# Gate, up and down as seven block products in place of eight, in three stages

## The chip, the cores and the metric

The kernel runs on one core of a Trainium2 chip. Such a core has a matmul engine, TensorE (PE in the profile; its weight loads, which overlap the matmuls, are PEld), and VectorE (DVE), ScalarE (ACT), GpSimd (POOL) and SyncE (SP), which run side by side, each through its own list of instructions in order, and wait for each other by semaphores. Operands lie in SBUF (128 partitions), matmuls write into PSUM (eight banks of 128 x 512 values), and 16 DMA engines move data between SBUF and DRAM. The metric is device time of one call in microseconds, the median of several runs.

## The reference

One layer of a decoder, for 2048 new prompt tokens and 8 decode tokens, all in float32. Two mixers (window attention and gated linear attention, GLA) give `mix` of 1024 columns; then comes what the change touches, with D_MODEL 1024 and D_FF 2816:

```python
def finish(x, o_attn, o_gla, r_gla, gla_norm_g, w_o, ffn_norm_g, w_gate, w_up, w_down):
    ...
    h = x + jnp.concatenate([o_attn.astype(x.dtype), g], axis=-1) @ w_o
    z = rmsnorm(h, ffn_norm_g)
    return h + (jax.nn.silu(z @ w_gate) * (z @ w_up)) @ w_down
```

## The kernel before

Every large product is made in three passes (`mm3`, lines 94 to 97): each float32 operand is split (`split`, L84 a cast on ACT, L85 a subtraction on DVE) into a high and a low part in a format of fewer bits that PE takes at its full rate, and high x high, high x low and low x high are added up in PSUM. So each operand that PE reads costs one ACT and one DVE pass over it, weights at every load.

The order of instructions on each engine is set by a scheduler ahead of time, from the order of the program and its own estimate of durations. A tile's buffer comes from a pool with a fixed number of them, so a load or a split waits until the last reader of an earlier tile is done. All loads and stores are issued from SP, whose list is in order too: a transfer that waits holds up those behind it.

The program has three phases.

*Phase A* makes the projections and window attention of 16 blocks of 128 tokens. *Phase B* is GLA, in eight rounds of two blocks: `front_b` (projections) and `gla_b` (the recurrence), and at the end of each block `mob`, the block's normalised output, is written to `mix_d` in DRAM (L853). Beside the last round runs `mixer_out_0` (L903): the first superblock's (512 tokens) product with `w_o`, into PSUM tiles `ps_wo`, added to x (`add_h`, L566), normalised, transposed by PE (`norm_T`) and split into `zT`. Its weights are loaded at L914.

*Phase C* (from L960) goes over four superblocks of 512 tokens; the decode tokens ride with the first, so that its columns are taken in `HALVES` of 256 and 264. D_FF is 22 blocks of 128, taken in `GROUPS` of 8, 8 and 6. For each group, `gate_up` (L1040) makes for each block the transposed products `pg` and `pu` (8 k tiles x 3 passes each, 512 columns), silu on ACT (L1057), the product on DVE (L1058) and the split `mid`; then `down` (L1065) multiplies `mid` with `w_down` into `ps_nat` and adds to `ht`, which holds h. For the first superblock `down_0` makes the product transposed (`ps_yT`) and `finish_0` turns it back (L1122). Between the two, in the last group, `mixer_out` makes h and `zT` of the next superblock. `unit` (L978) loads 512 KB of weights and splits them (tiles `wrc` and `hl`); gate, up and down are loaded again for each superblock.

Of the kernel before, what the change touches and what calls it, by code (L numbers as in the profile page):

```python
# [35 lines left out]
HALVES = ((0, 256), (256, 520))  # L36
GROUPS = ((0, 8), (8, 16), (16, 22))
# [7 lines left out]
def hymba_kernel(ctx: ExitStack, tc: tile.TileContext, I, O, X=None, phases=3):  # L45
# [25 lines left out]
    # the decode tokens' high parts in columns 0..7, low parts in columns 32..39  # L71
# [15 lines left out]
    def fold(ps, w, pool):  # L87
        """Sum of the two parts of a stacked decode product -> [8, w] in SBUF."""
# [5 lines left out]
    def mm3(ps, lh, ll, rh, rl, start, stop):  # L94
        nc.tensor.matmul(ps, lh, rh, start=start, stop=False)  # L95
        nc.tensor.matmul(ps, lh, rl, start=False, stop=False)  # L96
        nc.tensor.matmul(ps, ll, rh, start=False, stop=stop)  # L97
# [8 lines left out]
    def rstd_fast(ss, n, scale, cols):  # L106
        """(scale * ss + EPS) ** -0.5 by ln and exp, then one Newton step."""
# [26 lines left out]
    # ------------------------------------------------------------------ phase A  # L134
    with ExitStack() as ph:
# [21 lines left out]
        # resident projection weights of q_a k_a v_a lr, as exact high and low parts  # L157
# [30 lines left out]
        # per-partition gains of the transposed q and k  # L188
# [27 lines left out]
        def dense_dec(W, c0, c1):  # L216
            """The decode tokens' products: both parts of n stacked, two passes."""
# [8 lines left out]
        def gate_r(ps, n):  # L226
            """silu(r) of n tokens, with exp and ln only."""
# [10 lines left out]
        def head_norm(ps, n, c0, heads):  # L238
            """RMSNorm factors of the heads of 64 columns that start at column c0."""
# [7 lines left out]
        def norm_q(pq, n):  # L247
            r = head_norm(pq, n, 0, 8)
            qn = wk.tile([P, 512], F32, tag="qn", name="qn")
            # heads in the order (chunk, kv): chunk c holds heads c and 4 + c  # L250
# [25 lines left out]
        def project(b):  # L276
# [10 lines left out]
            # [v0 high, v0 low, v1 low, v1 high]  # L287
# [13 lines left out]
            # kv group 0: high rows 0..63, low rows 64..127; kv group 1 the other way round  # L301
# [84 lines left out]
        def decode_a():  # L386
            with ExitStack() as decs:
# [25 lines left out]
                # slots 0..126 hold the cached keys 1.., slot 127 the new key  # L413
# [69 lines left out]
        def make_bias():  # L483
            """Relative-position bias with the band mask, Toeplitz over (query, key)."""
            with tc.tile_pool(name="a_ext", bufs=1) as ep:
# [12 lines left out]
                # the queries in reverse order, turned round by a permutation  # L498
# [48 lines left out]

    # z^T of a superblock; in phase B its columns hold n^T of an even and of an odd pair of blocks
    late = pool(ctx, "late", 1, side="right")
    zT = late.tile([P, 2, KD, 520], F32R, name="zT")  # L550
    h_d = [dram.tile([P, D], F32, name=f"h_d{i}") for i in range(4)]
    hdec_d = dram.tile([ND, D], F32, name="hdec_d")
    w_o = I["w_o"][0]
# [640 lines left out]
```

## Time and profile before

| | us |
|---|---|
| median of three runs | 2439.91 (2439.74 to 2440.58) |
| span of the profiled execution | 2436.4 |
| median less span | 3.5 |
| first product with `w_o` starts | 721.1 |
| first gate product starts | 793.75 |
| last add of `down` starts | 2432.74 |

The profile is of one execution, and the runs' time holds some 3.5 us outside its span. In a row of a group stand its line, engine, operation, what it writes and reads, shapes and count, then its busy time and the mean of one in ns, and last the idle time of the engine before such instructions, with what ended it. In a row of a window stand start and end, its length, the busy time of PE, PEld, DVE, ACT and POOL with the number of instructions, the granted clock, the DMA engines' share and GB/s. In a timeline stand start, duration, engine and line; SPq is SP's issuing of transfers. Matmuls overlap each other: one of 512 columns is shown with 0.39 us, though they start some 0.23 us apart.

### The profile page before, as it was taken

The page shows a single profiled execution, that of the slowest core. Times are in us where ns is not written, and L with a number is a line of the kernel's source. Part 1 is how long each engine was busy: PE and PEld are TensorE (multiplying, and loading weights), DVE is VectorE, ACT ScalarE, POOL GpSimd, SP SyncE. Part 2 cuts the span into 40 slices and gives each one's busy share as a digit, 9 for nine tenths or more (in the row PEclk, how much of TensorE's full clock was granted, in tenths as well). Part 3 has the DMA queues.
Part 4 walks back from the last instruction along what each step waited for, and adds up shares of the span by engine and source line. Part 5 has one row for each costly group of instructions (what it writes and reads, how often), then busy time and mean ns, then how long its engine had stood idle before and what let it go on. Part 6 is the DMA issues. An engine that isn't in the chain of part 4 may idle for free.

```text
span 2436.4 us, 33308 instructions
## 1 busy us (share of the span) xinstructions
PE 2384.0 (98%) x13129; PEld 2039.6 (84%) x13129; DVE 1189.5 (49%) x2238; ACT 860.4 (35%) x1676; POOL 375.2 (15%) x460
## 2 busy tenths in 40 slices
PE   8998898999999999999999999999999999999999
PEld 6887787888887999999888888888888888888887
DVE  6886687787677433333443333353333334333332
ACT  5766677343343322222222222232222223222221
POOL 2543443654562000000000000000000000000000
PEclk9999999999999999999999999999999999999999
DMA  6423335433243523323454323354232333333231
GB/s 210 138 84 106 98 115 179 156 105 129 68 143 121 182 93 124 97 87 96 147 165 129 95 96 95 95 173 147 95 95 95 92 97 123 95 96 91 95 92 68
DMA packets 316636, 280.76 MB, mean 115 GB/s; under 512 B 11623, under 2 KB 263792, under 8 KB 314416
## 3 DMA queue, kind: packets, MB, share of 16 engines
q1 hardware_dynamic: 316480, 278.64, 36.4%
q8 instruction: 103, 1.69, 0.3%
q14 instruction: 53, 0.43, 0.1%
HBM read 228.80 MB, written 50.84 MB: 115 GB/s over the span
## 4 chain that ended last, share of the span: by engine, by line
PE 87%; DVE 5%; DMA 3%; POOL 2%; issue 1%; ACT 1%; SPq 0%; DVEq 0%; ACTq 0%; POOLq 0%
PE ps_nat L96 7%; PE ps_nat L95 7%; PE ps_nat L97 7%; PE pg L95 7%; PE pu L95 7%; PE pg L97 7%; PE pu L97 7%; PE pg L96 7%; PE pu L96 7%; PE ps_d L95 3%; PE ps_d L97 3%; PE ps_d L96 3%; PE ps_yT L95 2%; PE ps_yT L96 2%; PE ps_yT L97 2%; POOL bd L765 2%
## 5 line engine op out<-in xcount | busy, mean ns | idle before, releaser
L85 DVE TENSOR_TENSOR hl<-wrc,hl 128x1024 fp32r<-128x1024 f32 (+1 forms) x290 | 353.2, 1218 | 695.5 <-ACT hl L84 694.7
L84 ACT CAST hl<-wrc 128x1024 fp32r<-128x1024 f32 (+1 forms) x290 | 301.9, 1041 | 741.0 <-PE ps_nat L97 313.5
L95 PE MATMUL pg<-zT,hl 128*128 128x512 f32 (+2 forms) x880 | 308.7, 351 | 0.0
L95 PE MATMUL pu<-zT,hl 128*128 128x512 f32 (+2 forms) x880 | 308.3, 350 | 0.0
L97 PE MATMUL pg<-zT,hl 128*128 128x512 f32 (+2 forms) x880 | 308.0, 350 | 0.0
L97 PE MATMUL pu<-zT,hl 128*128 128x512 f32 (+2 forms) x880 | 308.0, 350 | 0.0
L96 PE MATMUL pg<-zT,hl 128*128 128x512 f32 (+2 forms) x880 | 307.0, 349 | 0.0
L96 PE MATMUL pu<-zT,hl 128*128 128x512 f32 (+2 forms) x880 | 306.8, 349 | 0.0
L103 POOL TENSOR_TENSOR rs_r<-rs_v,nhalf 128x1 f32<-128x1 f32 (+3 forms) x51 | 43.4, 855 | 1325.5 <-DVE rs_v L102 1324.8
L96 PE MATMUL ps_nat<-hl,mid 128*128 128x512 f32 x528 | 209.0, 396 | 0.0
L95 PE MATMUL ps_nat<-hl,mid 128*128 128x512 f32 x528 | 208.5, 395 | 0.0
L97 PE MATMUL ps_nat<-hl,mid 128*128 128x512 f32 x528 | 204.2, 393 | 0.0
L1058 DVE TENSOR_TENSOR sg<-sg,pu 128x512 f32<-128x512 f32 (+1 forms) x110 | 64.1, 583 | 251.5 <-PE pu L97 250.5
L96 PEld LDWEIGHTS pu<-zT,hl 128*128 128x128 f32 x880 | 165.4, 188 | 23.9
L97 PEld LDWEIGHTS pu<-zT,hl 128*128 128x128 f32 x880 | 165.4, 188 | 24.0
L97 PEld LDWEIGHTS pg<-zT,hl 128*128 128x128 f32 x880 | 165.4, 188 | 23.9
L96 PEld LDWEIGHTS pg<-zT,hl 128*128 128x128 f32 x880 | 165.4, 188 | 23.8
L95 PEld LDWEIGHTS pg<-zT,hl 128*128 128x128 f32 x880 | 165.4, 188 | 22.9
L95 PEld LDWEIGHTS pu<-zT,hl 128*128 128x128 f32 x880 | 165.2, 188 | 22.9
L1057 ACT ACTIVATE sg<-pg 128x512 f32<-128x512 f32 (+1 forms) x110 | 56.5, 514 | 353.8 <-PE pg L97 353.8
L765 POOL TENSOR_TENSOR bd<-E,qTb 64x128 f32<-64x128 f32 x224 | 127.2, 568 | 69.1 <-ACT E L753 54.2
L95 PEld LDWEIGHTS ps_nat<-hl,mid 128*128 128x128 f32 x528 | 99.0, 188 | 24.1
(347 smaller groups left out, 4758.0 us busy)
## 6 DMA issues: line engine op xcount, KB each, us to landing
wrc<-in_w_gate_dram SPq DMA_DIRECT2D x88, 512.0 KB
wrc<-in_w_up_dram SPq DMA_DIRECT2D x88, 512.0 KB
wrc<-in_w_down_dram SPq DMA_DIRECT2D x86, 512.0 KB
nT_d<-nT SPq DMA_DIRECT2D x16, 1024.0 KB
zT<-nT_d SPq DMA_DIRECT2D x8, 2048.0 KB
mt<-mix_d SPq DMA_DIRECT2D x12, 1024.0 KB
xt<-in_x_prompt_dram SPq DMA_DIRECT2D x16, 512.0 KB
mix_d<-mo SPq DMA_DIRECT2D x16, 512.0 KB
```

Of the source, the lines that this page charges most:

```text
L84: nc.scalar.copy(h, src)
L85: (eng or nc.vector).tensor_tensor(l, src, h.bitcast(F32), ALU.subtract)
L95: nc.tensor.matmul(ps, lh, rh, start=start, stop=False)
L96: nc.tensor.matmul(ps, lh, rl, start=False, stop=False)
L97: nc.tensor.matmul(ps, ll, rh, start=False, stop=stop)
L103: nc.gpsimd.tensor_tensor(r[:n, :cols], v[:n, :cols], nhalf[:n, :cols], ALU.pow)
L765: nc.gpsimd.tensor_tensor(bv[rows, :, h], eo, qo, ALU.mult)
L1057: nc.scalar.activation(sg[:, :w], pg[:, :w], AF.Silu)
L1058: nc.vector.tensor_tensor(sg[:, :w], sg[:, :w], pu[:, :w], ALU.mult)
```

## The change

Gate, up and down are each taken as a product of 2 x 2 blocks, by the Winograd form of Strassen's algorithm: seven products of sums of blocks, P1 to P7, in place of eight. The sums of activations are made once and kept, those of weights for each use, and the results are put together by adds. What was interleaved becomes three stages behind phase B. Phases A and B keep their work; `mixer_out_0` is gone from B.

*Stage M.* `w_o` is loaded once and stays split in SBUF (WO). Tiles of 128 tokens go in the order 0, 4, 1, 5 and so on: product, add, h to DRAM (`h_d`, L981), normalisation (with `rstd`, whose power is on POOL), transposes. For each two tiles that are four apart `operands` makes four sums and seven splits (`zhl`) and writes each, 512 KB in runs of 512 bytes, to `zc_d` by a DMA that POOL issues (L1016).

*Stage G.* Two superblocks of 1024 tokens, whose two blocks of rows are 512 tokens wide each (516 in the second, where the decode tokens ride, in two pieces of 258). The seven operands z are loaded once for a superblock (L1199, 2.1 MB each). For each of 11 pairs of D_FF blocks, gate and up have seven products of 4 k tiles x 3 passes each. `load_w` brings 4 x 512 KB of weights, `sums_a` their sums, `units` the splits (`whl`, seven buffers). `Strassen.ready` takes each finished product out of PSUM: P1 is copied by ACT; P6, P7, P5, P4 and P3 are added by DVE to what is there. P2 is added in PSUM onto P1, P7 and P4 onto P6, P3 onto P5; the eight banks go as three, three and two (tags a, b, c). In the first superblock gate's and up's products alternate; in the second all seven of gate come first. Four adds and subtractions make the seven operands of mid, which POOL writes to `md_d` (256 KB each, L1193).

*Stage D.* The pairs are taken in groups of 3, 3, 3 and 2. The 21 units of weights of a group are split once and kept (22 buffers). For each of eight pairs of row tiles the seven mid operands are loaded (`mr`, L1267) and split, and the four results of 128 x 512 are added to `h_d` in DRAM by a DMA with an add, which POOL issues; in the last group h is loaded (L1274), added, and written out. The decode tokens have products of their own (88 matmuls).

The diff, cut to what is new (`mixer_out_0` and the whole of phase C go, and the buffer of `zT` is now inside phase B):

```diff
-HALVES = ((0, 256), (256, 520))
-GROUPS = ((0, 8), (8, 16), (16, 22))
+GROUPS = ((0, 3), (3, 6), (6, 9), (9, 11))
+WIDTHS = (512, 516)
+PIECES = (((0, 512),), ((0, 258), (258, 516)))
+PRODS = ("P1", "P6", "P2", "P7", "P5", "P4", "P3")
...
-        mixer_out_0()
...
+        def operands(sb, mt, b):
...
+            sub(t1, b12, b11)
+            sub(t2, b22, t1)
+            sub(t3, b22, b12)
+            sub(t4, b21, t2)
+            for q, src in enumerate((b11, t2, b21, t3, t1, t4, b22)):
+                hl = hlp.tile([P, 2, 4, 132], F32R, tag="hl", name="zhl")
+                split(hl[:, 0, :, :w], hl[:, 1, :, :w], src)
+                nc.gpsimd.dma_start(zc_d[sb][q][:, :, :, mt * P:mt * P + w], hl[:, :, :, :w].bitcast(F32))
...
+    def sums_a(a11, a12, a21, a22):
+        yield a11
...
+        sub(x, a11, a21)
+        sub(y, a22, x)
+        yield y
+        yield a12
+        yield x
+        add(x, a21, a22)
+        yield x
+        yield a22
+        sub(y, a12, y)
+        yield y
...
+    BANK = {"P1": "a", "P2": "a", "P6": "b", "P7": "b", "P4": "b", "P5": "c", "P3": "c"}
...
+            if q == "P1":
+                nc.scalar.copy(p1, ps)
+            elif q == "P6":
+                add(u2, ps, p1)
+            elif q == "P7":
+                add(u3, ps, p1)
+            elif q == "P5":
+                add(u3, ps, u3)
+                self.done("22", i, u3)
+            elif q == "P4":
+                add(p1, ps, p1)
+                self.done("21", i, p1)
+            elif q == "P3":
+                add(u2, ps, u2)
+                self.done("12", i, u2)
+            elif q == "P2":
+                self.done("11", i, ps)
...
+            def prod(st, q, hl):
+                z = zc[q]
+                hv = hl.rearrange("p s (k n) -> p s k n", k=4)
+                for i, (c0, c1) in enumerate(pieces):
+                    ps = st.bank(q, i)[:, :c1 - c0]
+                    for k in range(4):
+                        mm3(ps, hv[:, 0, k], hv[:, 1, k], z[:, 0, k, c0:c1], z[:, 1, k, c0:c1],
+                            q in ("P1", "P6", "P5") and k == 0, k == 3, q not in ("P1", "P6", "P5"))
+                    st.ready(q, i)
...
+            add(s1, m12, m22)
+            sub(s2, s1, m11_)
+            sub(s3, m11_, m12)
+            sub(m12, m21, s2)
+            g = next(g for g, (p0, p1) in enumerate(GROUPS) if p0 <= fp < p1)
+            for q, src in enumerate((m11_, s2, m21, s3, s1, m22, m12)):
+                nc.gpsimd.dma_start(md_d[sb][g][:, :, q, fp - GROUPS[g][0], :], src.rearrange("p (m t) -> p m t", m=4))
...
+                    if last:
+                        add(hq[which], c, hq[which])
+                        nc.gpsimd.dma_start(O["y_prompt"][0, ti * P:(ti + 1) * P, cols], hq[which])
+                        return
+                    if which == "11":
+                        nc.scalar.copy(c11, c)
+                        c = c11
+                    nc.gpsimd.dma_start(h_d[ti][:, cols], c, accum_op=ALU.add)
```

Three places show how the engines' lists change. The first is SP's list at the end of phase B, before: `mix_d<-mob` writes a finished block, `wro` is a load of `w_o`, `zT<-mix_d` loads mix of a tile, `h_d<-ws` stores h.

```order
L853 DMA mix_d_83<-mob 256x1x512
L914 DMA wro<-in_w_o_dram 128x2x512
L914 DMA wro<-in_w_o_dram 64x2x512 x4
L914 DMA wro<-in_w_o_dram 128x2x512
L909 DMA zT<-mix_d_74 128x16x128
L914 DMA wro<-in_w_o_dram 128x2x512
L909 DMA zT<-mix_d_75 128x16x128
L725 DMA r<-r_d_113 128x512
L853 DMA mix_d_84<-mob 256x1x512
```

The same place after the change, from the last but one block on:

```order
L863 DMA mix_d_86<-mob 256x1x512
L922 DMA out_gla_state_prompt_dram<-Sbd 64x128 x2
L967 DMA h<-in_x_prompt_dram 128x1024 x2
L863 DMA mix_d_87<-mob 256x1x512
L955 DMA wro<-in_w_o_dram 64x2x512 x4
L955 DMA wro<-in_w_o_dram 128x2x512 x2
```

The loads of `w_o` stood ahead of the last four blocks' writes; now they stand behind the last of them.

The second is POOL's list in the middle of stage M. Before, POOL's list ends with the last rows of phase B (`qk`, `kd`), and behind them it has only the powers of the normalisations:

```order
L782 TENSOR_TENSOR qk<-qTb,kTb 128x512
L799 TENSOR_TENSOR kd<-kd,kTb 128x512
L103 TENSOR_TENSOR rs_r<-rs_v,nhalf 128x4 x2
L103 TENSOR_TENSOR rs_r<-rs_v,nhalf 128x1 x4
L103 TENSOR_TENSOR rs_r<-rs_v,nhalf 8x1
L103 TENSOR_TENSOR rs_r<-rs_v,nhalf 128x1 x12
```

After, for two tiles (`zc_d_P_` and a number is the DRAM tensor of one of the seven operands):

```order
L1016 DMA zc_d_P_4885<-zhl 1024x1x128
L111 TENSOR_TENSOR rs_r<-rs_v,nhalf 128x1
L1016 DMA zc_d_P_4886<-zhl 1024x1x128
L1016 DMA zc_d_P_4887<-zhl 1024x1x128
L1016 DMA zc_d_P_4888<-zhl 1024x1x128
L1016 DMA zc_d_P_4889<-zhl 1024x1x128
L111 TENSOR_TENSOR rs_r<-rs_v,nhalf 128x1
L1016 DMA zc_d_P_4890<-zhl 1024x1x128
L1016 DMA zc_d_P_4891<-zhl 1024x1x128
```

A tile's power now stands in the list behind transfers of 1024 runs, each of which waits for its split.

The third is DVE's list in the second superblock of stage G, where gate's products are taken out of PSUM (`gu` and `gp` are u2, u3 and p1 of gate, `ps_b` and `ps_c` PSUM tiles):

```order
L932 TENSOR_TENSOR sy<-wrg,sy 128x512
L92 TENSOR_TENSOR whl<-wrg,whl 128x512
L935 TENSOR_TENSOR gu_15559<-ps_b,gp_15557 128x258 x2
L92 TENSOR_TENSOR whl<-sx,whl 128x512
L935 TENSOR_TENSOR gu_15559<-ps_c,gu_15559 128x258
L935 TENSOR_TENSOR sx<-wrg 128x512
L935 TENSOR_TENSOR gu_15559<-ps_c,gu_15559 128x258
L92 TENSOR_TENSOR whl<-sx,whl 128x512
L935 TENSOR_TENSOR gp_15557<-ps_b,gp_15557 128x258
```

Between the adds that free PSUM (or the tile that the next product is added onto) stand the sums and splits of later weights, which themselves wait for ACT and for a buffer of `units`.

## What is predicted

> **What bounds the kernel now.** First the page of the profile of before: busy time by engine, the slices, and the chain that ended last.
>
> ```profile
> span 2436.4 us, 33308 instructions
> PE 2384.0 (98%) x13129; PEld 2039.6 (84%) x13129; DVE 1189.5 (49%) x2238; ACT 860.4 (35%) x1676; POOL 375.2 (15%) x460
> ...
> PE   8998898999999999999999999999999999999999
> ...
> DVE  6886687787677433333443333353333334333332
> ...
> PEclk9999999999999999999999999999999999999999
> ...
> PE 87%; DVE 5%; DMA 3%; POOL 2%; issue 1%; ACT 1%; SPq 0%; DVEq 0%; ACTq 0%; POOLq 0%
> ```
>
> From slice 14 on, PE is full, at full clock, and DVE stands at three or four tenths. The chain is PE for 87%. So the last two thirds, which the change replaces, are matmul time and nothing else: fewer matmul columns are time saved, as long as what is added stays beside PE. To price a column, take that whole stretch. These rows of the timeline are its first matmul of gate, its last matmul and the last add; the row of the chain prices eight transposes; and the last row, of the tile ps_wo, ends the first superblock's W_o.
>
> ```profile
> 793.75 0.28 PE L95 MATMUL pg<-zT,hl 128*128 128x256 f32 x1
> ...
> 2432.30 0.40 PE L97 MATMUL ps_nat<-hl,mid 128*128 128x512 f32 x1
> 2432.74 0.69 DVE L566 TENSOR_TENSOR ht<-ps_nat,ht 128x512 f32<-128x512 f32 x1 [0.71 <-PE ps_nat L97]
> ```
>
> ```profile
> 1193.86 0.87 PE ps_nT L130 x8
> ```
>
> ```profile
> L927 PE MATMUL ps_wo<-WV,mixdec x8: 390/393/397, 795.7 to 797.3; 128*40 128x512 f32 x8
> ```
>
> Counted from the loops, between the end of the first superblock's W_o (797.3 + 0.4 us; its decode tile overlaps the first gate matmuls) and that last matmul stand: for gate and up 3168 matmuls of 512 columns, 1056 of 264 and 1056 of 256; for down 1584 of 512 and 528 each of 264 and 256; for W_o of three superblocks 576 of 512. That is 3,551,616 columns, and 136 transposes of 0.87 / 8 us (14.8 us). (2432.7 - 797.7 - 14.8) / 3,551,616 = 0.456 ns a column: **0.2335 us for 512 columns, 0.1177 us for 258**. Do short matmuls pay extra? The two rows below are 18 matmuls of 264 columns apart, 0.1206 us each, 0.457 ns a column: no.
>
> ```profile
> 819.82 0.28 PE L96 MATMUL pu<-zT,hl 128*128 128x264 f32 x1
> ...
> 821.99 0.28 PE L96 MATMUL pu<-zT,hl 128*128 128x264 f32 x1
> ```
>
> **The change: matmuls.** All of it on PE:
> - stage M, W_o of 16 tiles and the decode tile: 768 + 32 matmuls x 0.2335 = 186.8, and 16 x 0.87 = 13.9 of transposes: 200.7 us, as before;
> - stage G, first superblock: 11 pairs x 2 x 7 products x 4 x 3 = 1848 x 0.2335 = 431.5; second: 3696 x 0.1177 = 435.0;
> - stage D: 8 x 11 x 7 x 3 = 1848 and 88 for the decode tokens, x 0.2335 = 452.1.
>
> Together **1519 us** of PE. The same work before: 1635.0 for the stretch above and 224 x 0.2335 + 4 x 0.87 = 55.8 for the first superblock's W_o, 1691 us. PE saves **172 us**, 7.1% of the span. What follows is what is given back.
>
> **Phase B to M.** SyncE's writes of finished blocks of mix, and three windows (us, then busy time and count of PE, PEld, DVE, ACT and POOL):
>
> ```profile
> 693.34 0.52 SPq L853 DMA_DIRECT2D mix_d<-mob  x1
> ...
> 739.12 0.55 SPq L853 DMA_DIRECT2D mix_d<-mob  x1
> ...
> 779.66 0.56 SPq L853 DMA_DIRECT2D mix_d<-mob  x1
> ```
>
> ```profile
> 720.00:740.00 20.00, 17.80 (x96) 14.68 (x95) 16.69 (x38) 7.41 (x17) 13.80 (x19) 1.00 0.29 93
> 740.00:760.00 20.00, 19.38 (x107) 15.63 (x107) 14.02 (x30) 5.82 (x15) 10.10 (x15) 1.00 0.21 79
> 760.00:780.00 20.00, 20.00 (x99) 16.62 (x98) 12.94 (x33) 5.76 (x15) 3.62 (x5) 1.00 0.31 114
> ```
>
> The last four blocks of phase B run between 693.3 and 779.7 us with the first superblock's W_o in their gaps. That filling goes: W_o's loads now stand behind the last mix_d write. Alone, the four blocks can't end before the DVE work in them allows (31 of the 40 us from 720 on; some 50 us counted from 693, so 743) nor later than now (780); I take the middle, 761. Then mix of one tile and the first unit of W_o (1.5 MB), a split and the first matmul: 8 us, so M starts at **769**. This is the largest loss: before, the first superblock's W_o was done at 797.7, mostly inside those gaps.
>
> **Inside M.** Durations of DVE, ACT and POOL from the groups by form:
>
> ```profile
> L85 DVE TENSOR_TENSOR mid<-sg,mid 128x512 fp32r<-128x512 f32 x66 | 45.2, 685 | 0.0
> L566 DVE TENSOR_TENSOR ht<-ps_nat,ht 128x512 f32<-128x512 f32 x96 | 64.0, 687 | 41.5 <-PE ps_nat L97 41.5
> L1058 DVE TENSOR_TENSOR sg<-sg,pu 128x264 f32<-128x264 f32 x22 | 9.5, 430 | 5.7 <-PE pu L97 5.7
> L125 DVE SCALAR_TENSOR_TENSOR z<-ht,rs_r,gBc 128x1024 f32<-128x1024 f32 x12 | 15.4, 1282 | 14.9 <-issue 12.5 <-PE ps_nT L130 2.3
> L84 ACT CAST mid<-sg 128x512 fp32r<-128x512 f32 x66 | 40.5, 613 | 0.0
> L122 ACT ACTIVATE zT<-ht 128x1024 fp32r<-128x1024 f32 x12 | 12.6, 1051 | 5.7 <-DVE ht L566 5.7
> L103 POOL TENSOR_TENSOR rs_r<-rs_v,nhalf 128x1 f32<-128x1 f32 x32 | 19.5, 617 | 1254.4 <-DVE rs_v L102 1254.0
> L103 POOL TENSOR_TENSOR rs_r<-rs_v,nhalf 128x32 f32<-128x32 f32 x1 | 5.4, 5429 | 0.1
> ```
>
> For each pair of tiles PE needs 2 x (48 x 0.2335 + 0.87) = 24.2 us. DVE: 4 adds, 4 sums, 7 subtractions and 2 copies of 512 at 0.685, two z at 1.28: 14.2 us. DMA: 4.2 MB of mix, x and h in long rows and 3.7 MB of operands in rows of 512 bytes. The rates are in two windows (share of the DMA engines, GB/s, at the end of each row):
>
> ```profile
> 808.00:816.00 8.00, 8.00 (x69) 8.00 (x69) 3.12 (x4) 2.97 (x5) 0.00 (x0) 1.00 1.00 417
> 1400.00:1440.00 40.00, 40.00 (x174) 32.31 (x173) 13.20 (x15) 11.57 (x16) 0.00 (x0) 1.00 0.29 93
> ```
>
> Full engines moved 417 GB/s; rows of 512 bytes (the weights in the second window) 93 / 0.29 = 320. So 10.1 + 11.5 = 21.6 of 24.2 us: hidden, but barely; I add 9 us for the first tile (eight units of W_o to split) and the decode tile.
>
> The Trainium skill, DMA: Bandwidth & Descriptors, section Bandwidth, gives about 358 GB/s for HBM per core where the neighbour is busy too; by that the z loads below would take 41 us for 35, and the sum would be 6 us longer. The trace has 417, which decides.
>
> POOL's seven transfers for each pair of tiles have no row: before, POOL issues none. Bounds for one issue: 0.52 us, what SyncE's queue shows for a mix_d write of the same 512 KB, and 5.43 us, POOL's longest instruction above. I take the first, since its row is the same transfer: 3.6 of 24.2 us. The upper end is a rival.
>
> **M to G.** The seven z operands (14.7 MB) lie over M's buffers, so they load when the last pair of tiles is done: normalisation (add 0.69, square 1.05, pow 0.62, z 1.28, transposes 0.87, copy 0.69, and what lies between: 6 us), sums and splits (6 us), the first 2.1 MB and its latency (7 us): 19 us without PE. Then 35 us of loads, with 3.7 MB of late operand writes beside them, feed a first pair that takes PE 39 us: 9 more. **28 us**.
>
> **Inside G.** A pair of blocks is 39.2 us on PE in the first superblock. DVE: 14 subtractions, 8 weight sums, 10 evacuations, 4 products, 4 sums, 40 x 0.685 = 27.4 us (70%). In the second superblock 28 of these become halves of 258 columns at 0.430 in place of 14 at 0.685: 29.9 of 39.6 us. ACT: 14 casts and 6 copies or silu, 12 us. All hidden, at nothing; before, DVE stood at 35% here, so the cover is thinner, and where it tears is the second rival.
>
> **G to D and D.** 8 us to load and split the first 21 units and mid products. A product group of one pair of row tiles takes 7 x 3 x 3 x 0.2335 = 14.7 us. At each of three group changes DVE makes 21 new units (33 operations, 22.6 us, beside 14 splits of 384 columns and 10 evacuations) in the 29 us that two such groups take: I allow 5 us each, 15. In the last group (two pairs, 9.8 us) DVE has 7 splits, 9 adds, 9 us with waits: 6 us over eight groups. Tail, last adds and writes: 5 us.
>
> An accumulating transfer has no row either. Plain, the four of 256 KB cost 1.05 MB / 417 = 2.5 us of the DMA's 14.7, next to 4.2 for the mid load (1.38 MB) and weights. From 4.2 times plain on (10.5 us) it would bind; below that it costs nothing. It is a plain write and a read, so I take twice.
>
> **Sum.** 769 + 200.7 + 9 + 28 + 866.5 + 8 + 452.1 + 15 + 6 + 5 = 2359.3 us of span. Before, the span is 2436.4 and the median of the runs 2439.9; the same 3.5 us outside gives **2363 us**, 3.2% faster.
>
> **Rivals.**
> 1. *POOL's issue binds M* (the slower side). For: rstd's pow stands in the same queue between the transfers, and 1024 runs of 512 bytes each may cost software more than SyncE. Against: SyncE's 0.52. The point is 24.2 / 7 = 3.46 us; at 5.43 a pair of tiles takes 38 us, 8 x 13.8 = 110 more: 2473. The gain is gone at 4.8 us. 18%.
> 2. *DVE's queue binds G.* P7 adds onto P6's bank, so PE waits until DVE has read P6; in the second superblock that leaves one piece and P2, 1.4 + 2.8 = 4.2 us. Ahead of such a read stand subtractions that wait for ACT and for one of seven unit buffers that PE frees. If one wait of 4 us is lost for each pair there, 44 us: 2407; in both superblocks 2451. 14%.
> 3. *Accumulation binds D.* At 5.5 times plain: 13.8 + 4.2 = 18 us for 14.7, 24 x 3.3 = 79: 2442. 8%.
> 4. *The joins cost half*, since the last blocks of B end by 743 and loads run ahead: 2330. 8%.
>
> Beside rival 1, the Trainium skill, SBUF — State Buffer, section Who interferes with whom, has a rule against this change: a transfer issued by GpSimd needs ports that VectorE's instructions can hold, and one stalled by VectorE is cured by another issuer. If issue ran only while DVE is idle, (24.2 - 14.2) / 7 = 1.4 us would be the point in place of 3.46, an estimate by that page; no run here shows it yet.
>
> **Numbers.** The forecast (2335 to 2400) gets 52%. Faster: 52, 8 of case 4, 11 of case 2, 4 of case 1, 3 of case 3: 78%. Within 0.2% (about what a measurement of this kernel can tell from no change, 2435 to 2445): 5%. Slower: 12 of case 1, 4 of case 3, 1 of case 2: 17%. The range 2330 to 2450 leaves out the upper part of cases 1 and 3 (about 14%) and little below.
>
> **What would show it.** The first W_o matmul near 769 and M 200 to 215 us long; over 230 with PE waiting for rs_r or hl buffers is case 1. G's pairs 39 to 40 us apart with PE full; PE idle before P7 with ps_b as releaser is case 2. D's groups 14.7 us apart; PE waiting for mr or h_d is case 3. A column rate other than 0.456, or phases A and B longer than now, would make the whole sum wrong.

## The result, and the profile after

| | before | after |
|---|---|---|
| median of four runs, us | 2439.88 (2439.74 to 2440.58) | 2361.27 (2359.49 to 2362.33) |
| ratio, with its 95% interval | | 0.9678 (0.9664 to 0.9691) |
| the profiled execution: its time, its span | 2439.9, 2436.4 | 2362.3, 2360.5 |

The change makes the kernel 3.2% faster. The forecast was 2363. It lies so near partly because errors of opposite sign cancelled, which the table in the section on the steps shows. First the page of the profile of after: busy time of the engines, and the slices.

```profile
span 2360.5 us, 34826 instructions
PE 2232.5 (95%) x12649; PEld 1925.1 (82%) x12649; DVE 1592.8 (67%) x3236; ACT 949.7 (40%) x2120; POOL 633.2 (27%) x807
...
PE   8998988799998799769999999999999989999998
...
DVE  6786867677777555627666666766767674848477
...
PEclk9999999799998899879999999999999999999999
DMA  6422324424221799893242429233323457878877
...
issue 51%; PE 20%; POOL 11%; DMA 8%; DVE 7%; ACT 2%; SPq 0%; POOLq 0%; ACTq 0%; DVEq 0%
```

PE lost 152 us of busy time, and the span only 76: there are now gaps. The new ones behind slice 12 stand in the PE row at 13 and 14 (the end of phase B) and 17 and 18 (from M to G), and the granted clock dips there (and in slice 8). DVE went from three or four tenths to six or seven behind phase B, and the DMA engines are nearly full in M and busy in D. The chain of the page, PE for 87% before, is now followed through POOL's list and put down to "issue" for half of the span. That doesn't show the bound here, since PE is 95% busy. The windows show it by stage (start, end, length; then busy time and count of PE, PEld, DVE, ACT, POOL; granted clock, DMA share, GB/s):

```profile
740.00:760.00 20.00, 13.22 (x69) 12.34 (x68) 18.30 (x39) 5.85 (x15) 13.15 (x20) 0.69 0.19 64
760.00:780.00 20.00, 9.42 (x40) 7.10 (x39) 8.96 (x28) 4.85 (x19) 2.01 (x2) 0.67 0.36 125
820.00:985.00 165.00, 164.59 (x783) 134.57 (x783) 94.17 (x152) 51.15 (x89) 48.44 (x61) 1.00 0.95 311
1100.00:1400.00 300.00, 300.00 (x1292) 242.58 (x1292) 199.66 (x308) 92.52 (x154) 38.80 (x55) 1.00 0.35 105
1500.00:1800.00 300.00, 300.00 (x2503) 300.00 (x2502) 203.82 (x398) 101.97 (x227) 35.68 (x50) 1.00 0.33 99
1940.00:2290.00 350.00, 350.00 (x1542) 284.44 (x1541) 219.69 (x386) 139.00 (x274) 85.07 (x102) 1.00 0.81 189
2020.00:2040.00 20.00, 20.00 (x90) 15.80 (x89) 19.71 (x35) 12.78 (x25) 5.12 (x6) 1.00 0.89 240
```

The first two are the end of phase B: PE has little to do, and its granted clock is 0.69 and 0.67. The next five are M, G's two superblocks, D, and one of D's changes of group. PE is full in each of them. Divide length by count and three different rates come out: 300 / 1292 = 0.2322 us a matmul in G's first superblock, 300 / 2503 = 0.1199 for 258 columns, 350 / 1542 = 0.2270 in D, though the first and the last are both of 512 columns. The experiments follow that up.

### The profile page after: what moved, and what is told of

Read it like the earlier page. It is cut to its first block, busy times and chain, and to the rows that moved or that the text cites. A ratio compares the mean times of both kernels' runs of the same rounds, so it can differ in the third digit from the quotient of the medians.

```text
span 2360.5 us, 34826 instructions
## 1 busy us (share of the span) xinstructions
PE 2232.5 (95%) x12649; PEld 1925.1 (82%) x12649; DVE 1592.8 (67%) x3236; ACT 949.7 (40%) x2120; POOL 633.2 (27%) x807
## 4 chain that ended last, share of the span: by engine, by line
issue 51%; PE 20%; POOL 11%; DMA 8%; DVE 7%; ACT 2%; SPq 0%; POOLq 0%; ACTq 0%; DVEq 0%
POOL md_d L1193 5%; DMA zc_d_P<-zhl 4%; POOL h_d L1286 3%; PE ps_d L103 3%; PE ps_d L105 3%; PE ps_d L104 3%; POOL bd L775 1%; PE ps_p L382 1%; PE ps_v L103 1%; PE ps_v L104 1%; PE ps_v L105 1%; POOL out_y_prompt_dram L1281 1%; DVE AT L788 1%; DMA Vc<-vod 1%; PE ps_l L780 1%
## 5 line engine op out<-in xcount | busy, mean ns | idle before, releaser
L104 PE MATMUL ps_b<-z,whl 128*128 128x258 f32 (+1 forms) x792 | 253.4, 320 | 0.0
L103 PE MATMUL ps_b<-z,whl 128*128 128x258 f32 (+1 forms) x792 | 253.0, 320 | 0.0
L105 PE MATMUL ps_b<-z,whl 128*128 128x258 f32 (+1 forms) x792 | 252.1, 318 | 0.0
L103 PE MATMUL ps_a<-z,whl 128*128 128x258 f32 (+1 forms) x528 | 170.1, 322 | 26.3 <-DMA z<-zc_d_P 26.3
L104 PE MATMUL ps_a<-z,whl 128*128 128x258 f32 (+1 forms) x528 | 170.1, 322 | 0.0
L105 PE MATMUL ps_a<-z,whl 128*128 128x258 f32 (+1 forms) x528 | 169.8, 322 | 0.0
L104 PE MATMUL ps_c<-z,whl 128*128 128x258 f32 (+1 forms) x528 | 169.1, 320 | 0.0
L105 PE MATMUL ps_c<-z,whl 128*128 128x258 f32 (+1 forms) x528 | 168.9, 320 | 0.0
L103 PE MATMUL ps_c<-z,whl 128*128 128x258 f32 (+1 forms) x528 | 168.5, 319 | 0.0
L105 PEld LDWEIGHTS ps_b<-z,whl 128*128 128x128 f32 x792 | 148.8, 188 | 12.0
L103 PEld LDWEIGHTS ps_b<-z,whl 128*128 128x128 f32 x792 | 148.9, 188 | 11.8
L104 PEld LDWEIGHTS ps_b<-z,whl 128*128 128x128 f32 x792 | 148.8, 188 | 11.8
L91 ACT CAST whl<-wrg 128x512 fp32r<-128x512 f32 x132 | 81.6, 620 | 153.0 <-PE ps_b L105 83.3
L103 PEld LDWEIGHTS ps_a<-z,whl 128*128 128x128 f32 x528 | 100.4, 190 | 34.9 <-DMA z<-zc_d_P 26.7
L1193 POOL DMA_DIRECT2D md_d<-m x22 | 15.6, 710 | 389.3 <-DVE m L1156 376.1
L935 DVE TENSOR_TENSOR gu<-ps_c,gu 128x512 f32<-128x512 f32 (+1 forms) x130 | 77.8, 599 | 58.1 <-PE ps_c L105 57.4
L92 DVE TENSOR_TENSOR whl<-wrg,whl 128x512 fp32r<-128x512 f32 x132 | 90.8, 689 | 37.4 <-ACT whl L91 37.0
L103 PE MATMUL ps_wo<-WO,mt 128*128 128x512 f32 x256 | 102.2, 400 | 9.8 <-ACT WO L91 9.8
L104 PEld LDWEIGHTS ps_a<-z,whl 128*128 128x128 f32 x528 | 100.1, 190 | 8.1
L103 PEld LDWEIGHTS ps_c<-z,whl 128*128 128x128 f32 x528 | 99.8, 189 | 8.0
```

The source lines that it names most:

```text
L91: nc.scalar.copy(h, src)
L92: (eng or nc.vector).tensor_tensor(l, src, h.bitcast(F32), ALU.subtract)
L103: nc.tensor.matmul(ps, lh, rh, start=start, stop=False, skip_group_check=more)
L104: nc.tensor.matmul(ps, lh, rl, start=False, stop=False, skip_group_check=more)
L105: nc.tensor.matmul(ps, ll, rh, start=False, stop=stop, skip_group_check=more)
L935: nc.vector.tensor_tensor(out, a, b, ALU.add)
```

## The experiments

Times are medians; the kernel before, run beside each, took 2439.4 to 2441.1. "The change" is the kernel after as it is, 2361.27. Diffs are against it unless told otherwise, and cut to what matters (`...`). Where a difference is under 5 us, the 95% intervals overlap, and the rows of the trace carry the reading, not the medians.

### What the saved product is worth: the third product twice

```diff
+                    for k in range(4 if q == "P3" else 0):
+                        mm3(ps, hv[:, 0, k], hv[:, 1, k], z[:, 0, k, c0:c1], z[:, 1, k, c0:c1], False, k == 3, True)
...
+                    for pi in range(npr if name == "P3" else 0):
...
+                        mm3(ps, hl[:, 0, cs], hl[:, 1, cs], w[:, 0], w[:, 1], False, pi == npr - 1, True)
```

> P3's matmuls are made twice in each set of seven, in gate, up and down, so that PE has the work of eight products while loads, sums, splits and transfers stay those of seven (P3 counts twice in the outputs). Theory, PE sets the time in G and D and the saved product is saved whole: 264 x 0.2325 + 528 x 0.120 + 264 x 0.2267 = 185 us more, 2546. That is 106 over the kernel before, what three stages cost beside the products. Rival, G or D is paced by VectorE or by transfers: under 150 us more, under 2511.

Measured 2544.21, ratio 1.0425 (1.0403 to 1.0447), 183 us over the change. By the rates above, the added matmuls are 264 x 0.2322 + 528 x 0.1199 + 264 x 0.2270 = 184.5 us. So the eighth product costs PE's whole time for it, and leaving it out saves all of that. It also shows the other side: with the matmuls of eight products (loads, sums and splits stay those of seven) the three stages are 104 us slower than the kernel before. The change is a gain of 183 and a loss of some 105.

### Does the accumulation bind D: a plain write in its place

```diff
-                    nc.gpsimd.dma_start(h_d[ti][:, cols], c, accum_op=ALU.add)
+                    nc.gpsimd.dma_start(h_d[ti][:, cols], c)
```

> The transfers of stage D that add into h in DRAM become plain writes of the same bytes (so h and the groups before the last are left out of the sum). Theory, the accumulation (178 us per thousand packets of 2 KB against 84 for plain ones) is hidden beside PE: within 5 us of 2361, only the DMA engines' share between 1940 and 2290 us falls from 0.81 to under 0.65. Rival, it holds up stage D through the buffers that it reads: 15 us or more faster.

Measured 2363.05, ratio 0.9684 (0.967 to 0.9699): the same as the change. POOL's queue in the stretch from 1940 to 2290 us (packets, MB, share of the DMA engines), of the change:

```profile
q0 software_dynamic: 13920, 25.29, 45.9%
...
h_d<-gu POOLq DMA_DIRECT2D x47, 256.0 KB, 4.9
```

and with the plain write:

```profile
q0 software_dynamic: 7952, 25.53, 18.9%
...
h_d<-gu POOLq DMA_DIRECT2D x48, 256.0 KB, 2.6
```

The same bytes cost 2.4 times as much of the DMA engines with the add, and land in 4.9 us in place of 2.6. All of it is hidden: the engines' share in D is 0.81 with the add and 0.54 without, and PE is full with both. The forecast took "twice" and put the point at 4.2 times, so this term was right, and the third rival is excluded.

### POOL's issue, or SyncE's, for the operands in M

```diff
-                nc.gpsimd.dma_start(zc_d[sb][q][:, :, :, mt * P:mt * P + w], hl[:, :, :, :w].bitcast(F32))
+                nc.sync.dma_start(zc_d[sb][q][:, :, :, mt * P:mt * P + w], hl[:, :, :, :w].bitcast(F32))
```

> The 56 operand writes of stage M are issued by SyncE in place of GpSimd. Theory, GpSimd's issue (0.87 us each, 6 of 24 us for two tiles) is hidden and VectorE doesn't hold it up: no faster than 2356; slower if the writes, each of which waits for its split, hold up the mix loads behind them in SyncE's list. Rival, by the Trainium skill's rule that a transfer issued by GpSimd is held up by VectorE: stage M is 10 us or more shorter, 2351 or less.

Three groups of POOL's issues in the change (mean of one in ns behind the busy time): the operands, accumulating writes, and one of mid's operands.

```profile
L1016 POOL DMA_DIRECT2D zc_d_P<-zhl x56 | 48.1, 871 | 121.8 <-DVE zhl L92 121.8
L1286 POOL DMA_DIRECT2D h_d<-gu x48 | 41.2, 858 | 127.7 <-DVE gu L935 110.4 <-DVE ty L935 7.1 <-DVE mhl__18923 L92 6.2
...
L1193 POOL DMA_DIRECT2D md_d<-m x22 | 15.6, 710 | 389.3 <-DVE m L1156 376.1 <-DVE whl L92 13.2
```

One issue is 0.87 us, above the 0.52 that the forecast took and far below the 3.46 at which it would bind M; POOL waits for DVE (121.8 us ahead of these issues), and DVE for POOL's powers only 2.2 us from 820 to 985 us. That excludes the first rival. Handing the writes to SyncE made the kernel slower than the change: 2379.69, ratio 0.9745 (0.9724 to 0.9766). The W_o matmuls of M run from 784.6 to 985.8 us in the change, 201 us, and here from 787.6 to 1005.6, 218 us. The queues in M (820 to 985 us), of the change:

```profile
q1 hardware_dynamic: 5604, 26.95, 48.5%
q0 software_dynamic: 6625, 24.15, 46.3%
```

and with SyncE's writes:

```profile
q1 hardware_dynamic: 46900, 47.04, 97.1%
```

Issued by POOL, 24.15 MB went in 6625 packets, 3.6 KB each, though the rows in DRAM are 512 bytes long. Issued by SyncE, the packets are about 1 KB on the mean with all loads counted in, and the engines, full in both, moved 47.0 MB in place of 51.1 in the same 165 us. PE then waits for loads of mix (6.1 us in this stretch, none before). SyncE's list also stands still for splits now (45.7 us from 784 to 1012 ahead of these writes); how much of the 18 us comes from the order of its list and how much from the smaller packets, no run separates. The rule that the prediction weighed (the Trainium skill, SBUF — State Buffer, section Who interferes with whom: a GpSimd-issued transfer held up by VectorE is cured by another issuer) finds no case here: with DVE busy for 94 of 165 us, POOL's issue takes 0.87 us and holds nobody up for long, and the other issuer costs 18 us.

### W_o's loads ahead of the end of phase B

```diff
+    craw = pool(ctx, "c_raw", 4)
...
-    craw = pool(ctx, "c_raw", 4)
```

The pool of raw weights, opened at the start of phase C in the change, is opened ahead of phase B here, so that its buffers lie over nothing that B uses and the loads and splits of W_o can go ahead of B's end.

> The buffers of raw weights are reserved ahead of phase B, so that W_o's loads need not wait for phase B's memory and stand ahead of the last four blocks' writes in SyncE's list. Theory, of the 15.6 us by which stage M starts later than predicted, the part from the last mix write to the first matmul (776.7 to 784.6) and the slow first units is W_o's load and split: M starts at 776 to 778, 2350 to 2354. Rival, M is paced by its transfers (95% of the DMA engines' time) from the start and the first operands come no sooner: 2358 or more.

Measured 2355.17, ratio 0.965 (0.9635 to 0.9664), 6 us less. The timeline of the change shows what starts M (start, duration; SPq is SyncE issuing):

```profile
776.70 0.56 SPq L863 DMA_DIRECT2D mix_d<-mob  x1
...
783.48 1.04 ACT L91 CAST WO<-wro 128x1024 fp32r<-128x1024 f32 x1 [7.59 <-DMA wro<-in_w_o_dram]
...
784.58 0.79 PE L103 MATMUL ps_wo<-WO,mt 128*128 128x512 f32 x1 [9.81 <-ACT WO L91]
```

and of this kernel:

```profile
780.30 0.56 SPq L864 DMA_DIRECT2D mix_d<-mob  x1
...
780.33 0.79 PE L103 MATMUL ps_wo<-WO,mt 128*128 128x512 f32 x1 [1.96 <-DVE mob L863]
```

In the change PE waits 7.9 us from B's last write to the first W_o matmul, for a load and a split; the forecast took 8. Here nothing is left between the two: the first matmul of M is released by DVE's last `mob`. What is left is that B's last write is no earlier than before (779.7 us then, 776.7 in the change, 773 to 783 in all the runs); the section on the steps shows where that comes from.

### The loads of z: room in the order in which they become free

```diff
-            for q, name in enumerate(PRODS):
+            for q, name in reversed(list(enumerate(PRODS))):
...
+            for q, name in enumerate(PRODS):
                 nc.sync.dma_start(zc[name].bitcast(F32), zc_d[sb][q])
```

The tiles of the seven z operands are laid out in the reverse order, and loaded in the order of use. The operand needed first then lies where M's buffers are free earlier.

> The seven z buffers are reserved in reverse order, so that P1's operand, which the first product reads, lies over W_o (last read by the last W_o matmul, 986 us) and not over the buffers of the last splits (1009 us). Theory, the join M to G is a wait for memory: P1's load is issued near 990 in place of 1009, the first product starts near 998 in place of 1021.6, and the run takes some 23 us less: 2338. Rival, the join is paced by the 3.7 MB of operand writes that still drain: the first product starts no earlier than 1015 and the run takes 2355 to 2361.

Measured 2358.47, ratio 0.9654 (0.9633 to 0.9675), 3 us less than the change, not clear of the noise, and far from the 2338 of the theory that the wait is one of place. PE's wait between M and G (from 985 to 1060 us) in the change:

```profile
PE ps_a L103 <- DMA z<-zc_d_P: 26.3, 1, 26.3
```

and in this kernel:

```profile
PE ps_a L103 <- DMA z<-zc_d_P: 10.8, 2, 6.9
...
PE ps_b L103 <- DMA z<-zc_d_P: 3.3, 1, 3.3
```

G's first matmul came 17 us earlier (1004.8 for 1021.6), but the second superblock only 4 (1449.8 for 1453.7): SyncE came to the end of the z loads at 1040 us in the change and at 1037 here, so the first products wait one by one. The 14.7 MB of z have to come in before the first pair is through, whichever comes first.

### Where the columns' rate comes from

G's first superblock and D run matmuls of the same shape at different rates. The z tiles have rows of 516 values of which 512 are used in the first superblock; the operand that is streamed in D lies in rows of 512. A trace holds no addresses; where a row begins follows here from the sizes of the tiles. Three edits test whether the start of a row decides. First, rows of 512 in a tile of 8 x 516, so that only every second z buffer begins at a multiple of 256 bytes:

```diff
-                zc[name] = zcp.tile([P, 2, 4, 516], F32R, tag=f"z{q}", name=f"z{q}")[:, :, :, :WIDTHS[sb]]
+                zt = zcp.tile([P, 8 * 516], F32R, tag=f"z{q}", name=f"z{q}")
+                zc[name] = zt[:, :8 * WIDTHS[sb]].rearrange("p (s k n) -> p s k n", s=2, k=4)
```

> In the first superblock of stage G the z operands lie with rows of 512 values behind each other in place of 516; nothing else changes. In the run of the change, matmuls of 512 columns start 0.2325 us apart in stage G, with a step that depends on the row of z that they read, and 0.2267 apart in stage D, evenly. Theory, the pitch of 516 costs it: the steps of the first superblock fall to 0.227, 1848 x 0.0058 = 11 us: 2350. Rival, it is the stage (what else runs beside it, or which operand is streamed): steps stay at 0.2325 and the time within 2 us of 2361.

Measured 2357.79, ratio 0.9661 (0.9646 to 0.9675), 3.5 us less. Its timeline shows why: these rows are the first matmul of gate's and up's P5, the first of P4 behind them, and one of P4 later.

```profile
1201.55 0.40 PE L103 MATMUL ps_c<-z,whl 128*128 128x512 f32 x1
...
1207.14 0.39 PE L103 MATMUL ps_b<-z,whl 128*128 128x512 f32 x1
...
1211.91 0.39 PE L103 MATMUL ps_b<-z,whl 128*128 128x512 f32 x1
```

24 matmuls of P5 take 5.59 us, 0.2329 each; 21 of P4 take 4.77, 0.2271. Three of the seven products, P6, P7 and P4, had become fast: each second buffer. The second edit makes the tile 4160 values (16640 bytes, 65 x 256), so that all seven begin at such a multiple:

```diff
...
+                zt = zcp.tile([P, 4160], F32R, tag=f"z{q}", name=f"z{q}")
...
```

> As the run with rows of 512 behind each other in the first superblock of stage G, but each z buffer also takes 16640 bytes, a multiple of 256, in place of 16512 (an odd multiple of 128). In the run before, only P6, P7 and P4 (every second buffer) had even steps of 0.227; P1, P2, P5 and P3 had 0.233. Theory, what counts is that the streamed row begins on a multiple of 256 bytes: now all seven have 0.227, 1848 x 0.0058 = 11 us less than the change: 2350. Rival, it is the PSUM bank (P6, P7 and P4 are those of tag b): steps and time stay as in the run before, 2358.

Measured 2347.85, ratio 0.9629 (0.9608 to 0.965), 13 us less. Its window of G:

```profile
1100.00:1400.00 300.00, 300.00 (x1325) 248.43 (x1324) 203.03 (x314) 94.77 (x157) 39.87 (x56) 1.00 0.35 106
```

1325 matmuls in place of 1292, so 1848 x (0.2322 - 0.2264) = 10.7 us of the 13 are the rate. The rest has another cause that both expectations left out: without the gap of 4 values, a partition's rows lie behind each other, and z is loaded in large packets. The queue of the loads, from 1022 to 1044 us in the change (packets, MB, share of the DMA engines):

```profile
q1 hardware_dynamic: 4242, 8.56, 104.6%
```

and from 1018 to 1040 us in this run:

```profile
q1 hardware_dynamic: 635, 9.36, 100.0%
```

PE's wait for the first z is 23.5 us here (23.6 in the run before) and 26.3 in the change. The third edit goes the other way and spoils D, with rows of 516 for its weights:

```diff
-                    hl = wdp.tile([P, 2, 512], F32R, tag="w", name="dhl")
+                    hl = wdp.tile([P, 2, 516], F32R, tag="w", name="dhl")[:, :, :512]
```

> The other way round: in stage D the split units of w_down, which are streamed, lie with rows of 516 values in place of 512 (4128 bytes each); nothing else changes. Theory, the row's place costs: the steps of stage D rise from 0.2267 to about 0.2325, 1848 x 0.0058 = 11 us: 2372. Rival, stage D is even because of what else runs there: 0.2267 and 2361.

Measured 2372.66, ratio 0.9726 (0.9706 to 0.9746), 11 us more, and D's window has 1510 matmuls for 1542:

```profile
1940.00:2290.00 350.00, 350.00 (x1510) 279.42 (x1509) 216.06 (x378) 136.78 (x269) 83.31 (x99) 1.00 0.79 182
```

350 / 1510 = 0.2318 us. So where the streamed rows begin is the cause, in both directions and in one and the same kernel from one buffer to the next. The kernel before has it too: its `zT` has rows of 520. Rows of 512 there for superblocks 1 to 3 (diff against before):

```diff
-    zT = late.tile([P, 2, KD, 520], F32R, name="zT")
+    zf = late.tile([P, 2 * KD * 520], F32R, name="zT")
+    zT = zf.rearrange("p (s k n) -> p s k n", s=2, k=KD)
+    zS = zf[:, 0:2 * KD * 512].rearrange("p (s k n) -> p s k n", s=2, k=KD)
```

> The kernel before, with z of the superblocks 1 to 3 in rows of 512 behind each other in place of 520 (the first superblock keeps 520); nothing else. Theory, the place of the streamed row costs the kernel before as much as the change: its 3168 gate and up matmuls of 512 columns step by 0.227 in place of 0.2327, 18 us less: 2422. Rival, it costs only beside the change's other work: 2438 to 2441.

Measured 2421.75, ratio 0.992 (0.9908 to 0.9932), 18 us less than before; 3168 matmuls of gate and up there times the 0.0058 us between P5 and P4 is 18.4. These rows are the first and last of 24 matmuls of `up` in this kernel, and two of `down` that are 24 apart:

```profile
1500.23 0.39 PE L95 MATMUL pu<-zT,hl 128*128 128x512 f32 x1
...
1505.44 0.39 PE L97 MATMUL pu<-zT,hl 128*128 128x512 f32 x1
...
1880.00 0.40 PE L95 MATMUL ps_nat<-hl,mid 128*128 128x512 f32 x1
...
1885.57 0.39 PE L95 MATMUL ps_nat<-hl,mid 128*128 128x512 f32 x1
```

`up` steps by 5.21 / 23 = 0.2265 us, and `down`, whose operand was not touched, still by 5.57 / 24 = 0.2321, though its streamed weights lie in rows of 512 too. So the length of a row is not enough; where the buffers of `down` begin, no trace shows, and no run moved them.

### All together, and the best kernel

The reversed order, aligned z and the early loads at once, and the second superblock in pieces of 256 and 260 columns, each with rows of its own:

```diff
-PIECES = (((0, 512),), ((0, 258), (258, 516)))
+PIECES = (((0, 512),), ((0, 256), (256, 516)))
...
+            for q, name in reversed(list(enumerate(PRODS))):
+                zt = zcp.tile([P, 4160], F32R, tag=f"z{q}", name=f"z{q}")
...
```

> The change with what the runs so far allow: z buffers of 16640 bytes with rows of 512 in the first superblock and, in the second, the pieces 0 to 256 and 256 to 516 each in rows of their own (so the first piece's rows begin on multiples of 256 bytes, the second's of 260 do not), raw weight buffers reserved ahead of phase B, and the z buffers in reverse order. Theory, the three add up: 13 us (aligned first superblock) and 6 (early W_o) and 3 (reverse order) as measured, and 1848 x 0.006 = 11 for the aligned halves of the second: 2361 - 33 = 2328. Rival, the join M to G is paced by its transfers, so what M gains by starting earlier is waited for there, and short matmuls don't gain: 2340 to 2348.

Measured 2353.03 (2345.14 to 2354.33; the profile is of the 2345.14), ratio 0.9634 (0.9619 to 0.9649), against 2328 expected. G's first matmul starts at 986.6 us, the earliest of all, and then the waits from 985 to 1060 us show a new one, PE's for ACT:

```profile
PE ps_a L103 <- ACT gp L1107: 24.8, 1, 24.8
ACT zhl L91 <- DMA zc_d_P<-zhl: 24.1, 4, 6.9
```

P2 is added onto P1's bank, and so waits for ACT's copy of P1. ACT's list is in order, and ahead of that copy stand the last splits of M's operands, each of which waits about 6 us until an earlier operand write has left its buffer (24.1 us in all, 9.2 in the change, 21.0 with the reversed order alone). Those writes now run beside z loads that are already under way, and landed 17.3 us after their issue (median of six; 5.0 of seven in the change). The wait between M and G was not removed; it went from the load of z to the writes of z. (More exactly than the next expectation puts it: the writes were delayed, not the loads, and ACT's order carried that to P1.) The new pieces gained nothing, which is 11 of the 25 us that are missing. These rows begin twelve matmuls of 256 columns, twelve of 260, and the next ones:

```profile
1599.96 0.28 PE L103 MATMUL ps_b<-z,whl 128*128 128x256 f32 x1
...
1601.39 0.28 PE L103 MATMUL ps_b<-z,whl 128*128 128x260 f32 x1
...
1602.84 0.28 PE L103 MATMUL ps_a<-z,whl 128*128 128x256 f32 x1
```

That is 0.1192 us each for 256 columns, though their rows begin at multiples of 256 bytes, and 0.1208 for 260: together no less than the 0.2397 of two pieces of 258.

Without the reversed order and the new pieces, aligned z and the early loads of W_o alone:

> Only the two edits that stood by themselves: z buffers of 16640 bytes with rows of 512 in the first superblock, and raw weight buffers reserved ahead of phase B; the z buffers in their old order, so that all seven loads start when the last splits are done. Theory, the run with everything lost 25 us at the third product because six loads in flight together delayed each other, and without that the two gains add up: 2361 - 13 - 6 = 2342. Rival, what M gains by starting earlier is lost at the join in any order: 2348.

Measured 2340.20 (2337.25 to 2343.72), ratio 0.9588 (0.9575 to 0.9601). It is the fastest whole kernel here, 21 us below the change and 4.1% below the kernel before. Against the kernel before with its own rows aligned, 2421.75, it is 3.4% faster (2340.2 / 2421.75, from two sets of runs). That kernel still takes 0.232 to 0.233 us for each matmul of `down` and of W_o; at D's rate these 1584 + 576 would save some 13 us more (2160 x 0.006, an estimate that no run tried).

### What the decode tokens' ride costs

The best kernel with the second superblock in one piece of 512, and the decode tokens' columns left out:

```diff
-PIECES = (((0, 512),), ((0, 258), (258, 516)))
+PIECES = (((0, 512),), ((0, 512),))
...
```

> As the run beside it, but the second superblock of stage G is taken in one piece of 512 columns, as the first, and the decode tokens' four columns for each block are left out (their part of mid is zero). Theory, matmuls of 258 columns are paced by the weight loads (PEld is busy 20.0 of 20 us there) at 0.120 us, so two cost 0.240 for one of 0.2267: 3696 x 0.120 - 1848 x 0.2267 = 25 us less than the run beside it, 2317. Rival, they are paced by their columns (516 x 0.443 ns = 0.2285): under 5 us less.

Measured 2317.26, ratio 0.9492 (0.9479 to 0.9505), 23 us less. Its window of that superblock, to set beside the one of the change above:

```profile
1500.00:1800.00 300.00, 300.00 (x1326) 248.47 (x1324) 202.65 (x316) 94.72 (x158) 39.64 (x55) 1.00 0.35 105
```

300 / 1326 = 0.2262 us for 512 columns, where two pieces of 258 take 0.2397. So 3696 x 0.1199 - 1848 x 0.2262 = 25 us go for four decode columns in each of the two blocks of rows. The expectation's reason, that short matmuls go at the pace of the weight loads, fits PEld's row (busy for 300.00 of 300.00 us in the change, 248 here), but is not shown: a load is shown with 0.19 us while one starts every 0.12, so the loads overlap, and no run changed the loads alone.

## Why the prediction was right, step by step

The sum of the prediction against the profiled execution:

| term, us | predicted | measured |
|---|---|---|
| M starts | 769 | 784.6 |
| M with its transposes | 209.7 | 210.4 (to 995.0) |
| M to G | 28 | 26.6 (to 1021.6) |
| G, first superblock | 431.5 | 432.1 (to 1453.7) |
| G, second superblock | 435.0 | 443.4 (to 1897.1) |
| join, D, changes of group, last group | 481.1 | 456.4 (to 2353.5) |
| tail | 5 | 7.0 |
| outside the span | 3.5 | 1.8 |
| sum | 2363 | 2362.3 |

**The main step held.** In G and D PE is full, in M from 820 us on as well, and each matmul left out is its time saved; the doubled product shows it with 183 us. The cover that the forecast counted on (DVE at 70% in G, DMA in M "hidden, but barely") was as thin as it said, with DVE at 67% (199.66 of 300) and the DMA engines at 95% in M for 89% forecast, and it did not tear.

**B's end did not come earlier: +15.6 us, and not by the length that was forecast.** The forecast took 761 for the last mix_d write, 68 us behind the twelfth block's at 693.3. These are SyncE's last five writes in the change (the second row holds two):

```profile
709.80 0.52 SPq L863 DMA_DIRECT2D mix_d<-mob  x1
739.83 15.13 SPq L863 DMA_DIRECT2D mix_d<-mob  x2
771.93 0.55 SPq L863 DMA_DIRECT2D mix_d<-mob  x1
776.70 0.56 SPq L863 DMA_DIRECT2D mix_d<-mob  x1
```

The last four blocks took 66.9 us, as forecast, and 86.3 before. But the twelfth block's write came at 709.8 in place of 693.3. Phase B kept its work, not its order in time: its first block was ready at 485 us for 496 before, its twelfth at 709 for 693. The step that failed is that everything ahead of the last four blocks was taken as unchanged. With W_o's loads early (four runs) the twelfth write comes at 693 to 702 again, and the last four take 79 to 81 us, so B ends between 773 and 783 in either order; why, is open. PE is busy for 19.64 of 20 us from 720 to 740 in the change, and behind that no engine is full, DVE with 18.30 of 20 until 760 the nearest. PE's granted clock fell there from 1.00 to 0.69 and 0.67; whether that slowed the chain, no run here tells apart.

**M to G was right in its sum, not in its parts.** From the last W_o matmul (986.3) to the last split took 22.8 us for 12 forecast; 8.7 of them, to the last transpose, stand under M in the table, in its margin of 9. Of the rest, 7.3 us are ACT's waits, ahead of the last four splits, for earlier operand writes to leave their buffers. From the last split to G's first matmul it took 12.5 us for 7. The 9 us for a first pair that starves did not come: behind the first matmul there is no wait for z. These errors cancel. That the wait is bandwidth rather than place, and moves when one end is shortened, the reversed order and the combination showed.

**Two rates.** "Do short matmuls pay extra? ... no" was wrong: 0.1199 us in place of 0.1177, +8.4 us. The two rows that it rested on gave 0.1206, but for 264 columns. Two rows of the same kernel, 17 matmuls of 256 columns apart, give 0.1194:

```profile
805.56 0.28 PE L95 MATMUL pg<-zT,hl 128*128 128x256 f32 x1
...
807.59 0.28 PE L97 MATMUL pg<-zT,hl 128*128 128x256 f32 x1
```

That is 0.466 ns a column for 0.457: with half the columns a matmul takes more than half the time, and a price per column fitted only the form that it was read from. D's matmuls went the other way: 1936 x (0.2335 - 0.2270) = 12.6 us less than forecast. Gate, up, `down` and W_o of before all step at 0.232 to 0.233, so that kernel has, behind 797 us, no kind of 512 columns at D's rate to read it from; the price carried the place of the old operands over to new ones.

**D's margins were not used.** 456.4 less 1936 x 0.2270 is 17 us for the join and everything else, where 8 + 15 + 6 = 29 were allowed. At a change of group DVE is busy for 19.71 of 20 us and PE still has no gap.

**The rivals.** POOL's issue (0.87 us for 3.46) and the accumulation (2.4 times for 4.2, and hidden) are excluded by their sizes. DVE's queue in G holds PE up nowhere, since PE is busy for all of both windows. It was ACT's queue, in the combination, where such a wait turned up. The fourth, cheap joins at 2330, was not the change, and no edit of the joins reached it: the sum of what was tried on them is some 9 us, of which 3 are not clear of the noise.

What stays open: why B ends at the same time in either order, what paces the short matmuls, and whether z's writes and loads can overlap without one starving the other. PE's gaps there, in the change 10 us ahead of M and 26 ahead of G, are the largest left.

## What to carry to other kernels

A product saved on a full engine is saved whole; what a restructuring costs is in its seams, so price those by the chain that has to run dry there, not by the work that used to fill its gaps. Take the rate of an engine form by form, and with the operands that it was measured on: where the rows lay moved it by 2.5%, and a price per column failed at half the columns. Where work is taken out of one phase, look whether the rest keeps its order in time before taking a start from the old trace. Where a wait for a transfer is removed by starting it earlier, look for what it then competes with, and for an in-order queue that passes the delay on.

## What the runs showed of the hardware

- Streamed rows of 512 values in the four-byte format took 0.2262 to 0.2271 us a matmul where each began at a multiple of 256 bytes, and 0.232 to 0.233 where not, 2.5% more; it showed from one buffer to the next in one kernel, and was worth 18 us to the kernel before.
- While z was loaded, the loads went at 427 GB/s in 635 packets for 9.36 MB where a partition's rows lie without gaps, and at 390 GB/s in 4242 for 8.56 MB with a gap of 16 bytes behind each row of 2 KB; PE's wait for the first z was 23.5 us for 26.3.
- Matmuls of 256 to 264 columns with a weight load each went at 0.119 to 0.121 us wherever their rows began, with PEld busy all the time: more than half of what 512 columns took.
- An accumulating DMA took 2.4 times the DMA engines' time of a plain one (45.9% for 18.9% of the same stretch).
- POOL's issue of 512 KB in 1024 rows of 512 bytes took 0.87 us and made packets of some 3.6 KB; the same transfers by SyncE went in smaller packets (1 KB on the mean with the loads) and moved 47.0 MB for 51.1 on full engines; the run took 18 us longer.
- Behind the wait between M and G, PE's granted clock was 0.50 and 0.66 in these windows, and full from 1030 us on, with z's loads at 335 to 391 GB/s:

```profile
1012.00:1022.00 10.00, 0.36 (x1) 0.36 (x2) 0.00 (x0) 0.00 (x0) 0.00 (x0) 0.50 1.02 335
1022.00:1030.00 8.00, 8.00 (x25) 6.30 (x25) 1.38 (x2) 1.11 (x2) 0.00 (x0) 0.66 1.05 389
1030.00:1040.00 10.00, 10.00 (x45) 8.12 (x44) 3.77 (x6) 4.74 (x7) 0.00 (x0) 1.00 1.05 391
```
